# The last product of w_down in PSUM banks of its own, and the last output row gathered in one tile

## The chip, the core and the metric

The kernel runs on one core of one Trainium2 chip. Five engines work side by side: PE (TensorE, the matrix products; PEld is its weight load), DVE (VectorE), ACT (ScalarE), POOL (GpSimd) and SP (SyncE, which here only starts DMAs). The metric is the device time of one execution in microseconds (us); lower is better.

## The reference, cut to what matters

One encoder layer on 512 rows of 1024 numbers, all float32: two mixers, a cross-attention, then a SwiGLU feed-forward part and a final norm. Only the end bears on the change:

```python
def rms_norm(x, g):
    y = xf * lax.rsqrt(jnp.mean(xf * xf, axis=-1, keepdims=True) + EPS)
    return y * g
...
h = h + (silu(hn @ w_gate) * (hn @ w_up)) @ w_down      # hn (512, 1024), D_FF = 2816
return rms_norm(h, final_norm_g)
```

## The kernel before

**Tiles.** The residual `h` lies in SBUF as four tiles of 128 rows ("rows 0 to 3", index `t`) by 1024 columns; `HALF[0]` and `HALF[1]` are columns 0:512 and 512:1024. Every float32 operand of a product is split into a coarse half (`hi`, an ACT cast) and a remainder (`lo`, a DVE subtraction; `split`, lines 85 and 86), and `mm3` (line 374) issues three matmuls, hi by hi, hi by lo and lo by hi, for each 128x128 by 128x512 piece.

**w_down by seven products.** The 512x2816 by 2816x1024 product is done by Strassen's scheme with seven half-sized products in the order `DOWN = (1, 5, 2, 6, 3, 7, 4)`. Each goes through w_down in six chunks `c`, the sixth half as deep as the others. `down_product` runs a product into a pair of PSUM banks, one bank for each of two rows; `onto_h` (line 1922) then adds or subtracts a pair onto half a column range of two rows of `h`. The pairs are `dx`, `dq` and `dv`, six of the eight banks. The line that the text calls "the switch" stands where product 7 ends and product 4 begins:

```python
    down_product(dx, 7, False)
    onto_h(dx, 2, 0, ALU.subtract)
```

Product 4 goes on accumulating in `dx`: its sum with what `dx` already holds is what columns 512:1024 of rows 2 and 3 need, while `dx` up to product 7 is what is subtracted from columns 0:512.

**Product 4 and its order.** Chunks 0 to 2 run for both rows. Chunks 3 to 5 are held back (`HELD = 3`): row 2 is finished first, then row 3 in two column pieces of 256 in the banks `dv`. `seed_last` (line 1890) puts `h` plus the half-done bank into `dv` ahead of that; line 1959 adds row 2's bank onto `h`.

**Weights on their way.** A chunk is loaded by SP into one of three buffers `wraw` (line 299), cast by ACT into one of three `whi` buffers, and subtracted by DVE into one of three `wlo` buffers. A `wraw` buffer is free when DVE's subtraction has read it; a `whi` buffer when PE's last matmul on it is through. Chunk 3 of product 4 so takes the buffers of chunk 0, chunk 4 those of chunk 1, chunk 5 those of chunk 2. SP starts the loads in order, each when its buffer is free, and behind the last of them four stores of rows 0 and 1 (line 1950).

**Final norm.** `first_half` squares and multiplies by the gain the half of a row that is done first, and keeps the product in `hg`, four slots of 512 columns at the end of the tile `rest`, slot `t` for row `t`. `finish` or `finish_last` takes the other half, `inv_root` makes one over the root of the mean square, `write` scales both halves and stores them. For row 3 `write` has ACT scale `hg` (line 1906, 512 columns), DVE scale `h` (line 1914, 512 columns), SP store the one half (line 1912) and ACT's queue the other (line 1917).

**Order.** Outside the passages marked `in_order` a scheduler sorts each engine's instructions by its own model; `in_order` pins an instruction to the program's order.

Of the kernel before, what the change touches and what calls it, by code (L numbers as in the profile page):

```python
# [11 lines left out]
AF = mybir.ActivationFunctionType  # L12
ALU = mybir.AluOpType
# [4 lines left out]
P = 128  # L18
D = 1024
T = 512  # L20
NT = T // P
# [31 lines left out]
def hybrid_layer_kernel(  # L53
# [8 lines left out]
    nc = tc.nc  # L62
    x, mem, out = x[0], mem[0], out[0]
# [13 lines left out]
    def bank(name):  # L77
        return pm.tile([P, 512], F32, tag="mm", name=name)

    def aux(name, shape=(P, 512)):  # L80
        return pa.tile(list(shape), F32, tag="aux", name=name)
# [12 lines left out]
    in_order = tc.keep_in_program_order  # L94
# [165 lines left out]
    DOWN, CHUNKS = (1, 5, 2, 6, 3, 7, 4), 6  # L260
# [85 lines left out]
    def next_w(*key):  # L346
        i = used_w[0]
        used_w[0] += 1
        assert len(plan[i][0]) == len(key) and plan[i][0][1:] == key[1:] and plan[i][0][0] is key[0]
        for j in range(i, min(i + FAR + 1, len(plan))):  # L350
            begin(j, i)
            if j - 1 >= len(tiles) and j - 1 <= i + SPLITS:
                split_w(j - 1)
        for j in range(len(tiles), min(i + SPLITS + 1, len(plan))):
            split_w(j)
        tile_, tiles[i] = tiles[i], None
        return tile_
# [13 lines left out]
    def mm3(ps, a, b, start, stop, free=False, turn=False):  # L371

        for i, (x, y) in enumerate(((0, 0), (0, 1), (1, 0))):
            m = nc.tensor.matmul(ps, a[x], b[y], start=start and i == 0, stop=stop and i == 2, skip_group_check=free)  # L374
            if turn:
                in_order(m)
# [90 lines left out]
    def tick(us=5.2):  # L467

        side["now"] += us / 5.2
        run_due()  # L470
        side["credit"] = min(side["credit"] + us * side["rate"], us)
        while side["credit"] > 0.0 and side["gen"] is not None:
            try:
                used = next(side["gen"])
            except StopIteration:
                side["gen"] = None
                return
            if used is None:
                side["credit"] = 0.0
                return  # L480
            side["credit"] -= used

    def gain(src, name, late=False):
        t = np_.tile([P, D], F32, tag="gain", name=name, bufs=2)
        load = nc.sync.dma_start(t, src.partition_broadcast(P))
        if late:
            in_order(load)
        return t
# [8 lines left out]
    def sum_sq(dst, src, sq=None, bias=0.0):  # L497
        if sq is None:
            sq = np_.tile([P, 512], F32, tag="ev", name="sq", bufs=2)
        act = nc.scalar.activation(sq[:, :src.shape[-1]], src, AF.Square, bias=bias, accum_out=dst)  # L500
        if pinned[0]:
            in_order(act)
# [11 lines left out]
    HALF = (slice(0, 512), slice(512, 1024))  # L514
# [39 lines left out]
    def slot(tag, shape, dt, name, place=NEAR):  # L554
        n = math.prod(shape[1:])
        t = sp.tile([P, KD * T + ROOM[tag]], dt, tag=tag, name=name)[:, place[tag]:place[tag] + n]
        return t.rearrange("p (a b c) -> p a b c", a=shape[1], b=shape[2]) if len(shape) == 4 else (
            t.rearrange("p (a b) -> p a b", a=shape[1]))
# [838 lines left out]
    h = slot("A", (P, NT, D), F32, "h")  # L1397
# [242 lines left out]
    scaled = {}  # L1640
# [153 lines left out]
    def rows_product(ps, q, c, ops_, ts, cs, start, stop, turn=False):  # L1794
        hi, lo = ops_
        a = made[q, c // 2]
        for t in ts:
            tsl = slice(t * P, (t + 1) * P)
            for k in range(hi.shape[1]):
                kk = 2 * (c % 2) + k  # L1800
                mm3(ps[t], (a[0][:, kk, tsl], a[1][:, kk, tsl]), (hi[:, k, cs], lo[:, k, cs]),
                    start and k == 0, stop and k == hi.shape[1] - 1, True, turn)
        tick(1.35 * len(ts))

    def down_product(ps, q, start, chunks=range(CHUNKS)):
        for c in chunks:
            rows_product(ps, q, c, next_w(w_down, q, c), (0, 1), slice(0, 512), start and c == 0, c == CHUNKS - 1,
                         chunks[0] == c > 0)

    for i, u in enumerate(UNITS):  # L1810
        final = i == len(UNITS) - 1
        x, v = begun
# [13 lines left out]
        else:  # L1826
            dx = [bank(f"dx{t}") for t in range(2)]
# [20 lines left out]

    g_o = gain(final_norm_g, "g_o")
    hg = rest[0][:, 4:8, :]  # L1850
    msq = fp.tile([P, NT + 2], F32, name="msq", bufs=1)

    def mean_sq(dst, ss, base):
        nc.vector.scalar_tensor_tensor(dst, ss, 1.0 / D, base, ALU.mult, ALU.add)

    early, HELD = {}, 3

    def first_half(t, half):

        early[t] = half  # L1860
        sum_sq(hss[:, 2, t, half:half + 1], h[:, t, HALF[half]])
        nc.vector.tensor_tensor(hg[:, t, :], h[:, t, HALF[half]], g_o[:, HALF[half]], ALU.mult)
        nc.vector.tensor_scalar(msq[:, t:t + 1], hss[:, 2, t, half:half + 1], 1.0 / D, EPS, ALU.mult, ALU.add)

    def inv_root(t, ss):
        r = np_.tile([P, 1], F32, tag="r", name="r", bufs=2)
        ms = np_.tile([P, 1], F32, tag="ms", name="ms", bufs=2)
        root = nc.scalar.activation(ms, ss, AF.Sqrt, bias=msq[:, t:t + 1], scale=1.0 / D)
        inv = nc.vector.reciprocal(r, ms)
        if pinned[0]:  # L1870
            in_order(root)
            in_order(inv)
        return r
# [11 lines left out]
    last = [dv[i][:, 0:256] for i in range(2)]  # L1885
    last_cols = [slice(512 + 256 * i, 768 + 256 * i) for i in range(2)]

    def seed_last(ps):
        for i in range(2):
            in_order(nc.vector.tensor_tensor(last[i], h[:, NT - 1, last_cols[i]], ps[:, 256 * i:256 * i + 256], ALU.add))  # L1890

    def finish_last(i):
        ss = np_.tile([P, 2], F32, tag="ss", name="ss", bufs=2)
        sum_sq(ss[:, 0:1], last[i])
        in_order(nc.vector.tensor_tensor(h[:, NT - 1, last_cols[i]], last[i], g_o[:, last_cols[i]], ALU.mult))
        if i == 0:
            mean_sq(msq[:, NT:NT + 1], ss[:, 0:1], msq[:, NT - 1:NT])
        else:
            write(NT - 1, inv_root(NT, ss[:, 0:1]))

    stores = []

    def write(t, r):
        rows = out[t * P:(t + 1) * P]
        cs, hs = HALF[early[t]], HALF[1 - early[t]]
        scaled = nc.scalar.activation(hg[:, t, :], hg[:, t, :], AF.Copy, scale=r)
        if t < 2:
            nc.vector.scalar_tensor_tensor(h[:, t, hs], h[:, t, hs], r, g_o[:, hs], ALU.mult, ALU.mult)
            stores.extend([(rows[:, cs], hg[:, t, :]), (rows[:, hs], h[:, t, hs])])
            return  # L1910
        in_order(scaled)
        nc.sync.dma_start(rows[:, cs], hg[:, t, :])
        if t == NT - 1:
            in_order(nc.vector.tensor_scalar(h[:, t, hs], h[:, t, hs], r, None, ALU.mult))
        else:
            in_order(nc.vector.scalar_tensor_tensor(h[:, t, hs], h[:, t, hs], r, g_o[:, hs], ALU.mult, ALU.mult))
        (nc.scalar if t == NT - 1 else nc.sync).dma_start(rows[:, hs], h[:, t, hs])

    def onto_h(ps, t0, half, op):
        for t in range(2):  # L1920
            hs = h[:, t0 + t, HALF[half]]
            nc.vector.tensor_tensor(hs, hs, ps[t], op)  # L1922

    dq = [bank("dq0"), aux("dq1")]
# [7 lines left out]
    for t in range(2):  # L1932
        first_half(t, 1)
# [5 lines left out]
        finish(t)  # L1939
    down_product(dx, 7, False)  # L1940
    onto_h(dx, 2, 0, ALU.subtract)
    for t in range(2, 4):
        first_half(t, 0)

    held = []
    for c in range(CHUNKS):
        ops_ = next_w(w_down, 4, c)
        if c == CHUNKS - 1 - LOADS:
            for dst, src in stores:
                in_order(nc.sync.dma_start(dst, src))  # L1950
        if c < CHUNKS - HELD:
            rows_product(dx, 4, c, ops_, (0, 1), slice(0, 512), False, c == CHUNKS - HELD - 1)
        else:
            held.append((c, ops_))
    seed_last(dx[1])
    for c, ops_ in held:
        rows_product(dx, 4, c, ops_, (0,), slice(0, 512), False, c == CHUNKS - 1, True)
    pinned[0] = True
    in_order(nc.vector.tensor_tensor(h[:, 2, HALF[1]], h[:, 2, HALF[1]], dx[0], ALU.add))
    finish(2)  # L1960
    for i in range(2):
        for c, ops_ in held:
# [36 lines left out]
```

## Time and profile before

| | us |
|---|---|
| median of 3 runs | 866.23 (866.2, 866.23, 868.49) |
| the profiled execution, its own time | 865.49 |
| its span, first to last instruction | 863.7 |
| PE busy | 856.1 |
| DVE busy | 660.5 |
| ACT busy | 466.1 |

The granted TensorE clock of the profiled execution is 0.998. A row of the timeline begins with the start and the duration in us, then engine, line, operation and "output<-inputs"; a time in brackets is how long the engine sat idle before it and what ended that. A matmul row's duration is longer than the distance to the next one, since matmuls overlap; rates are read from starts.

### The profile page before, as it was taken

The page shows a single profiled execution, that of the slowest core. Times are in us where ns is not written, and L with a number is a line of the kernel's source. Part 1 is how long each engine was busy: PE and PEld are TensorE (multiplying, and loading weights), DVE is VectorE, ACT ScalarE, POOL GpSimd, SP SyncE. Part 2 cuts the span into 40 slices and gives each one's busy share as a digit, 9 for nine tenths or more (in the row PEclk, how much of TensorE's full clock was granted, in tenths as well). Part 3 has the DMA queues.
Part 4 walks back from the last instruction along what each step waited for, and adds up shares of the span by engine and source line. Part 5 has one row for each costly group of instructions (what it writes and reads, how often), then busy time and mean ns, then how long its engine had stood idle before and what let it go on. Part 6 is the DMA issues. An engine that isn't in the chain of part 4 may idle for free.

```text
span 863.7 us, 14764 instructions
## 1 busy us (share of the span) xinstructions
PE 856.1 (99%) x5780; PEld 766.6 (89%) x5780; DVE 660.5 (76%) x1076; ACT 466.1 (54%) x698; POOL 89.3 (10%) x119
## 2 busy tenths in 40 slices
PE   9999999999999999999999999999999999999997
PEld 7888888888889988889899888999999999988886
DVE  7698896899846768668758755867877768899875
ACT  6734853244355543557547544645545554656674
POOL 0002302111021110110010001010211111000000
PEclk9999999999999999999999999999999999999999
DMA  9759565987574798735696555557999898366564
GB/s 270 196 174 308 113 174 153 254 195 191 146 220 150 244 309 248 244 102 199 213 276 162 147 146 147 146 159 185 213 233 240 215 229 220 92 191 209 196 186 156
DMA packets 115752, 169.56 MB, mean 196 GB/s; under 512 B 9297, under 2 KB 80481, under 8 KB 115554
## 3 DMA queue, kind: packets, MB, share of 16 engines
q1 hardware_dynamic: 95330, 139.54, 49.3%
q0 software_dynamic: 20064, 28.55, 20.4%
q8 instruction: 45, 0.74, 0.3%
q10 hardware_dynamic: 288, 0.52, 0.2%
q14 instruction: 25, 0.20, 0.1%
HBM read 159.71 MB, written 48.73 MB: 241 GB/s over the span
## 4 chain that ended last, share of the span: by engine, by line
PE 99%; DVE 1%; ACT 0%; issue 0%
PE pf L374 27%; PE pt L374 18%; PE px L1238 13%; PE dx L374 7%; PE pq L1238 6%; PE dq L374 3%; PE pv L1238 3%; PE bx L1238 3%; PE qx L1238 3%; PE dv L374 2%; PE pz L958 2%; PE qv L1238 1%; PE po L374 1%; PE psc L374 1%; PE py L1014 1%; PE qq L1238 1%
## 5 line engine op out<-in xcount | busy, mean ns | idle before, releaser
L85 ACT CAST whi<-wraw 128x1024 fp32r<-128x1024 f32 x141 | 145.2, 1031 | 160.2 <-PE pf L374 54.8
L86 DVE TENSOR_TENSOR wlo<-wraw,whi 128x1024 fp32r<-128x1024 f32 x141 | 168.3, 1195 | 64.8 <-ACT whi L85 64.2
L374 PE MATMUL pf<-xn,whi 128*128 128x512 f32 x448 | 140.1, 392 | 0.0
L374 PEld LDWEIGHTS pf<-xn,whi 128*128 128x128 f32 x448 | 83.5, 188 | 16.9
L374 PE MATMUL pf<-xn,wlo 128*128 128x512 f32 x224 | 87.5, 391 | 0.0
L1238 PE MATMUL px<-fn,whi 128*128 128x256 f32 x480 | 83.4, 277 | 0.0
L1238 PEld LDWEIGHTS px<-fn,whi 128*128 128x128 f32 x480 | 72.5, 188 | 0.2
L86 DVE TENSOR_TENSOR wlo<-b,whi 128x1024 fp32r<-128x1024 f32 x40 | 48.9, 1223 | 26.0 <-ACT whi L85 26.0
L85 ACT CAST whi<-b 128x1024 fp32r<-128x1024 f32 x40 | 42.2, 1054 | 48.3 <-PE px L1238 27.7
L1238 PE MATMUL px<-fn,wlo 128*128 128x256 f32 x240 | 66.4, 277 | 0.0
L1238 PE MATMUL pq<-s,whi 128*128 128x256 f32 x320 | 55.0, 276 | 0.0
L374 PE MATMUL dx<-whi,s 128*128 128x512 f32 x166 | 52.2, 391 | 0.4 <-DVE h L1922 0.4
L86 DVE TENSOR_TENSOR wlo<-t,whi 128x1024 fp32r<-128x1024 f32 x30 | 36.7, 1225 | 18.4 <-ACT whi L85 18.4
L85 ACT CAST whi<-t 128x1024 fp32r<-128x1024 f32 x30 | 31.6, 1054 | 34.6 <-PE pv L1238 11.4
L374 PEld LDWEIGHTS pf<-xn,wlo 128*128 128x128 f32 x224 | 42.1, 188 | 8.7
L1238 PEld LDWEIGHTS pq<-s,whi 128*128 128x128 f32 x320 | 48.2, 188 | 0.0
L1238 PEld LDWEIGHTS px<-fn,wlo 128*128 128x128 f32 x240 | 45.1, 188 | 0.0
L1238 PE MATMUL pq<-s,wlo 128*128 128x256 f32 x160 | 44.2, 276 | 0.0
L374 PE MATMUL pt<-whi,xn 128*128 128x512 f32 x128 | 43.1, 402 | 0.0
L374 PEld LDWEIGHTS dx<-whi,s 128*128 128x128 f32 x166 | 31.1, 188 | 7.4 <-ACT whi L85 0.8
L374 PE MATMUL dx<-wlo,s 128*128 128x512 f32 x83 | 32.2, 389 | 0.0
L289 POOL DMA_DIRECT2D dsum<-in_w_down_dram x12 | 13.2, 1103 | 172.5 <-DMA dsum<-in_w_down_dram 167.4
(458 smaller groups left out, 2222.7 us busy)
## 6 DMA issues: line engine op xcount, KB each, us to landing
wraw<-in_w_in_dram SPq DMA_DIRECT2D x34, 512.0 KB, 4.6
dsum<-in_w_down_dram SPq DMA_DIRECT2D x20, 512.0 KB, 5.8
wraw<-dsum SPq DMA_DIRECT2D x20, 512.0 KB, 4.4
b<-in_w_gate_dram SPq DMA_DIRECT2D x15, 512.0 KB, 5.1
b<-in_w_up_dram SPq DMA_DIRECT2D x15, 512.0 KB, 4.7
wraw<-in_w_down_dram SPq DMA_DIRECT2D x15, 512.0 KB, 3.8
dsum<-in_w_down_dram POOLq DMA_DIRECT2D x10, 512.0 KB, 7.5
dsum<-dsum POOLq DMA_DIRECT2D x10, 512.0 KB, 7.9
```

The source lines that it names most:

```text
L85: hi = nc.scalar.copy(dst_hi, src)
L86: lo = nc.vector.tensor_tensor(dst_lo, src, dst_hi.bitcast(F32), ALU.subtract)
L289: plan[j + step][1].append((0, lambda d=dst, x=more: nc.gpsimd.dma_start(d, x, accum_op=ALU.add)))
L374: m = nc.tensor.matmul(ps, a[x], b[y], start=start and i == 0, stop=stop and i == 2, skip_group_check=free)
L958: nc.tensor.matmul(ps[:, g, :], wt[:, g, :], u[:, o * GO + g, :], start=True, stop=True)
L1014: in_order(nc.tensor.matmul(ps[64 * j:64 * j + 64, :, :, h, :].rearrange("p q d c -> p d q c"), a, b, start=k == ks[0], stop=k == ks[2], t ...
L1238: nc.tensor.matmul(ps[:, j, :], a[x], b[y], start=start and j == k == i == 0, stop=k == 3 and i == 2, skip_group_check=True)
```

## The change

Product 4 gets the pair `dq`, which product 3 has long left, and starts it afresh. What `dx` holds at the switch is now added onto columns 512:1024 of rows 2 and 3 as well, by two more DVE additions next to the two subtractions. `seed_last` and line 1959 read `dq` in place of `dx`. Row 3 is gathered in one tile: `hg`'s slots are dealt out by `HG` so that row 3's first half lies in slot 1 and its second half goes to slot 2, where row 0's half was, which the store of line 1950 (now 1960) has to have read by then. A new function `write_last` scales columns 0:352 of it on ACT and 352:1024 on DVE, and stores these two parts, SP the narrow one and ACT's queue the wide one. Line numbers behind it move up by 3 to 10.

```diff
+    HG = (2, 3, 0, 1)
+    last_row = hg[:, 1:3, :].rearrange("p a c -> p (a c)")
+    CUT = 352
...
-        nc.vector.tensor_tensor(hg[:, t, :], h[:, t, HALF[half]], g_o[:, HALF[half]], ALU.mult)
+        nc.vector.tensor_tensor(hg[:, HG[t], :], h[:, t, HALF[half]], g_o[:, HALF[half]], ALU.mult)
...
-        in_order(nc.vector.tensor_tensor(h[:, NT - 1, last_cols[i]], last[i], g_o[:, last_cols[i]], ALU.mult))
+        in_order(nc.vector.tensor_tensor(last_row[:, last_cols[i]], last[i], g_o[:, last_cols[i]], ALU.mult))
...
-            write(NT - 1, inv_root(NT, ss[:, 0:1]))
+            write_last(inv_root(NT, ss[:, 0:1]))
...
+    def write_last(r):
+        rows = out[(NT - 1) * P:NT * P]
+        x, y = last_row[:, 0:CUT], last_row[:, CUT:D]
+        in_order(nc.scalar.activation(x, x, AF.Copy, scale=r))
+        in_order(nc.vector.tensor_scalar(y, y, r, None, ALU.mult))
+        nc.sync.dma_start(rows[:, 0:CUT], x)
+        nc.scalar.dma_start(rows[:, CUT:D], y)
...
     down_product(dx, 7, False)
     onto_h(dx, 2, 0, ALU.subtract)
+    onto_h(dx, 2, 1, ALU.add)
...
-            rows_product(dx, 4, c, ops_, (0, 1), slice(0, 512), False, c == CHUNKS - HELD - 1)
+            rows_product(dq, 4, c, ops_, (0, 1), slice(0, 512), c == 0, c == CHUNKS - HELD - 1)
...
-    seed_last(dx[1])
+    seed_last(dq[1])
     for c, ops_ in held:
-        rows_product(dx, 4, c, ops_, (0,), slice(0, 512), False, c == CHUNKS - 1, True)
+        rows_product(dq, 4, c, ops_, (0,), slice(0, 512), False, c == CHUNKS - 1, True)
...
-    in_order(nc.vector.tensor_tensor(h[:, 2, HALF[1]], h[:, 2, HALF[1]], dx[0], ALU.add))
+    in_order(nc.vector.tensor_tensor(h[:, 2, HALF[1]], h[:, 2, HALF[1]], dq[0], ALU.add))
```

The scheduler sorts the passage around the switch anew. PE's order there before; `dx0` is row 2's bank, `dx1` row 3's, `whi_8860` is chunk 5 of product 7, `whi_8881`, `whi_8899` and `whi_8924` are chunks 0, 1 and 2 of product 4, and `s` holds the tokens:

```order
L374 MATMUL dx1_8077<-whi_8860,s4_8837 128x512
L374 MATMUL dx0_8076<-whi_8881,s1_8878 128x512
L374 MATMUL dx0_8076<-wlo_8882,s1_8878 128x512
L374 MATMUL dx0_8076<-whi_8881,s1_8878 128x512 x2
L374 MATMUL dx0_8076<-wlo_8882,s1_8878 128x512
L374 MATMUL dx0_8076<-whi_8881,s1_8878 128x512
L374 MATMUL dx0_8076<-whi_8899,s1_8878 128x512
L374 MATMUL dx0_8076<-wlo_8900,s1_8878 128x512
L374 MATMUL dx0_8076<-whi_8899,s1_8878 128x512 x2
L374 MATMUL dx0_8076<-wlo_8900,s1_8878 128x512
L374 MATMUL dx0_8076<-whi_8899,s1_8878 128x512
L374 MATMUL dx0_8076<-whi_8924,s2_8921 128x512
```

Row 2 takes chunks 0 and 1 in full before row 3 begins. The same place after the change, with `dq0` and `dq1` for rows 2 and 3:

```order
L374 MATMUL dx1_8077<-whi_8860,s4_8837 128x512
L374 MATMUL dq0_8217<-whi_8881,s1_8878 128x512
L374 MATMUL dq1_8218<-whi_8881,s1_8878 128x512
L374 MATMUL dq0_8217<-wlo_8882,s1_8878 128x512
L374 MATMUL dq0_8217<-whi_8881,s1_8878 128x512 x2
L374 MATMUL dq0_8217<-wlo_8882,s1_8878 128x512
L374 MATMUL dq0_8217<-whi_8881,s1_8878 128x512
L374 MATMUL dq1_8218<-wlo_8882,s1_8878 128x512
L374 MATMUL dq1_8218<-whi_8881,s1_8878 128x512 x2
L374 MATMUL dq1_8218<-wlo_8882,s1_8878 128x512
L374 MATMUL dq1_8218<-whi_8881,s1_8878 128x512
L374 MATMUL dq0_8217<-whi_8899,s1_8878 128x512
```

Both rows now go through chunk 0 before chunk 1. DVE's order from the switch to the subtraction of chunk 4 before:

```order
L1922 TENSOR_TENSOR h_3612<-h_3612,dx0_8076 128x512
L86 TENSOR_TENSOR wlo_8900<-wraw_8876,whi_8899 128x1024
L1922 TENSOR_TENSOR h_3612<-h_3612,dx1_8077 128x512
L1862 TENSOR_TENSOR rest_7714<-h_3612,g_o_8212 128x512
L86 TENSOR_TENSOR wlo_8925<-wraw_8897,whi_8924 128x1024
L86 TENSOR_TENSOR s4_8960<-rest_7714,s4_8960 128x512
L86 TENSOR_TENSOR s4_8960<-pair_5661,s4_8960 128x256
L1862 TENSOR_TENSOR rest_7714<-h_3612,g_o_8212 128x512
L1863 TENSOR_SCALAR msq_8214<-hss_3624 128x1 x2
L86 TENSOR_TENSOR wlo_8943<-wraw_8919,whi_8942 128x1024
L86 TENSOR_TENSOR wlo_8966<-wraw_8940,whi_8965 128x1024
```

and after the change, where `wlo_8900`, `wlo_8927`, `wlo_8945` and `wlo_8968` are the remainders of chunks 1, 2, 3 and 4:

```order
L1931 TENSOR_TENSOR h_3612<-h_3612,dx0_8076 128x512 x2
L86 TENSOR_TENSOR wlo_8900<-wraw_8876,whi_8899 128x1024
L1931 TENSOR_TENSOR h_3612<-h_3612,dx1_8077 128x512 x2
L1865 TENSOR_TENSOR rest_7714<-h_3612,g_o_8212 128x512
L86 TENSOR_TENSOR wlo_8927<-wraw_8897,whi_8926 128x1024
L86 TENSOR_TENSOR s4_8962<-rest_7714,s4_8962 128x512
L86 TENSOR_TENSOR s4_8962<-pair_5661,s4_8962 128x256
L1866 TENSOR_SCALAR msq_8214<-hss_3624 128x1
L1865 TENSOR_TENSOR rest_7714<-h_3612,g_o_8212 128x512
L86 TENSOR_TENSOR wlo_8945<-wraw_8921,whi_8944 128x1024
L1866 TENSOR_SCALAR msq_8214<-hss_3624 128x1
L86 TENSOR_TENSOR wlo_8968<-wraw_8942,whi_8967 128x1024
```

One addition stands ahead of chunk 1's subtraction and two ahead of chunk 2's. On ACT the square of row 3's first half moves behind the cast of chunk 3. Ahead of the switch every engine's order is as it was.

More of the change, by code (lines that the diff above doesn't have):

```diff
@@ L1905, in write @@
         cs, hs = HALF[early[t]], HALF[1 - early[t]]
-        scaled = nc.scalar.activation(hg[:, t, :], hg[:, t, :], AF.Copy, scale=r)
+        hgt = hg[:, HG[t], :]
+        scaled = nc.scalar.activation(hgt, hgt, AF.Copy, scale=r)
         if t < 2:
             nc.vector.scalar_tensor_tensor(h[:, t, hs], h[:, t, hs], r, g_o[:, hs], ALU.mult, ALU.mult)
-            stores.extend([(rows[:, cs], hg[:, t, :]), (rows[:, hs], h[:, t, hs])])
+            stores.extend([(rows[:, cs], hgt), (rows[:, hs], h[:, t, hs])])
             return
         in_order(scaled)
[L1912 to L1917, printed above, removed]
+        nc.sync.dma_start(rows[:, cs], hgt)
+        in_order(nc.vector.scalar_tensor_tensor(h[:, t, hs], h[:, t, hs], r, g_o[:, hs], ALU.mult, ALU.mult))
+        nc.sync.dma_start(rows[:, hs], h[:, t, hs])
+    def write_last(r):
[5 more added lines that the diff above has]
+        nc.scalar.dma_start(rows[:, CUT:D], y)
     def onto_h(ps, t0, half, op):
```

## The prediction

> **What bounds the kernel now.** I read the page first: who is busy, and who makes up the chain that ended last.
>
> ```profile
> PE 856.1 (99%) x5780; PEld 766.6 (89%) x5780; DVE 660.5 (76%) x1076; ACT 466.1 (54%) x698; POOL 89.3 (10%) x119
> PE 99%; DVE 1%; ACT 0%; issue 0%
> ```
>
> PE is the bound. No engine's order changes ahead of the switch, so only the last 22 us can move. For them I asked for the chain of waits from 838 us on (start, duration, what):
>
> ```profile
> 837.89 3.87 PE dx L374 x17
> ...
> 841.78 0.70 DVE h L1922
> ...
> 842.62 11.84 PE dx L374 x51
> ...
> 859.12 0.72 ACT rest L1906
> ```
>
> PE leaves the chain twice: at the switch, where DVE's subtraction of row 2's `dx` bank stands between two matmuls, and at the end, where the last row is scaled and stored. The change touches both. PE's timeline at product 7's first matmul, its last one, the first of product 4 and the first and last on `dv`:
>
> ```profile
> 827.08 0.62 PE L374 MATMUL dx<-whi,s 128*128 128x512 f32 x2
> ...
> 841.81 0.39 PE L374 MATMUL dx<-whi,s 128*128 128x512 f32 x1
> 842.62 0.47 PE L374 MATMUL dx<-whi,s 128*128 128x512 f32 x1 [0.42 <-DVE h L1922]
> ...
> 854.30 0.28 PE L374 MATMUL dv<-whi,s 128*128 128x256 f32 x1
> ...
> 857.77 0.28 PE L374 MATMUL dv<-whi,s 128*128 128x256 f32 x1
> ```
>
> Product 7 has 66 matmuls, 65 distances: (841.81 - 827.08) / 65 = 0.2266 us each. Without a wait product 4 would start at 842.04; it starts at 842.62, 0.58 later. Its 51 wide matmuls then take 854.30 - 842.62 = 11.68 us, 0.2290 each, where 51 x 0.2266 = 11.56: another 0.12 lost after the stop.
>
> **Part 1: two fresh banks.** DVE's timeline has the last reading of `dq`, by line 1922 on product 3, and the remainder of product 4's chunk 0:
>
> ```profile
> 828.57 0.68 DVE L1922 TENSOR_TENSOR h<-h,dq 128x512 f32<-128x512 f32 x1
> ...
> 839.29 1.23 DVE L86 TENSOR_TENSOR wlo<-wraw,whi 128x1024 fp32r<-128x1024 f32 x1 [1.35 <-ACT whi L85]
> ```
>
> Both are done by 840.52, the cast of that chunk ahead of its remainder, so the first matmul of product 4 finds a free bank and its weights at 842.04. PE should run through: `dv` starts at 842.04 + 51 x 0.2266 = 853.60 instead of 854.30, a gain of 0.70. Its bounds are 0.42 (the idle time that the row itself shows) and 0.81 (the whole distance 841.81 to 842.62).
>
> **Part 2: two more additions on DVE.** They are queued ahead of the remainders that product 4 needs. DVE's timeline from the switch on:
>
> ```profile
> 841.78 0.69 DVE L1922 TENSOR_TENSOR h<-h,dx 128x512 f32<-128x512 f32 x1
> 842.39 1.22 DVE L86 TENSOR_TENSOR wlo<-wraw,whi 128x1024 fp32r<-128x1024 f32 x1
> 843.52 0.68 DVE L1922 TENSOR_TENSOR h<-h,dx 128x512 f32<-128x512 f32 x1
> 844.12 0.69 DVE L1862 TENSOR_TENSOR rest<-h,g_o 128x512 f32<-128x512 f32 x1
> 844.72 1.22 DVE L86 TENSOR_TENSOR wlo<-wraw,whi 128x1024 fp32r<-128x1024 f32 x1
> ...
> 846.80 0.68 DVE L1862 TENSOR_TENSOR rest<-h,g_o 128x512 f32<-128x512 f32 x1
> ...
> 848.37 2.59 DVE L86 TENSOR_TENSOR wlo<-wraw,whi 128x1024 fp32r<-128x1024 f32 x2 [0.77 <-ACT whi L85]
> 851.75 0.69 DVE L86 TENSOR_TENSOR wlo<-wraw,whi 128x512 fp32r<-128x512 f32 x1 [0.79 <-ACT whi L85]
> 852.36 0.75 DVE L1890 TENSOR_TENSOR dv<-h,dx 128x256 f32<-128x256 f32 x2
> ```
>
> An addition takes 0.60 from start to start (843.52 to 844.12), a remainder 1.13. In the new order chunk 1's remainder ends at 842.39 + 0.60 + 1.22 = 844.21, chunk 2's at 844.72 + 1.20 + 1.22 = 847.14. PE asks for them at its 15th and 27th matmul, 842.04 + 14 x 0.2266 = 845.21 and 842.04 + 26 x 0.2266 = 847.93: 1.0 and 0.8 spare. For chunk 3's remainder DVE was free from 848.37 - 0.77 = 847.60 on; 1.20 later is 848.80, and it ends at 850.02; PE asks at its 38th, 850.42: 0.4 spare. The 0.77 and 0.79 us that DVE sat idle before take up the additions.
>
> For this chunk 3's cast must come sooner than it did. ACT's timeline (the casts of chunks 3 and 5), then SP's loads of chunks 4 and 5 with the time from issue to landing of each, from the answer on the tile `wraw` in a window round each:
>
> ```profile
> 847.29 1.05 ACT L85 CAST whi<-wraw 128x1024 fp32r<-128x1024 f32 x1 [1.93 <-issue]
> ...
> 851.10 0.62 ACT L85 CAST whi<-wraw 128x512 fp32r<-128x512 f32 x1 [1.39 <-PE dx L374]
> ...
> 843.63 0.32 SPq L299 DMA_DIRECT2D wraw<-dsum  x1
> DMA to landing us min/median/max: 4.4/4.4/4.4
> ...
> 845.97 0.32 SPq L299 DMA_DIRECT2D wraw<-dsum  x1
> DMA to landing us min/median/max: 4.0/4.0/4.0
> ```
>
> Before, row 3's chunk 0 stood 13 matmuls late in PE's order, and the cast at 847.29 waited for its buffer till then. Now chunk 0 is through after 12 matmuls, near 845.0, about when chunk 3's load lands; the cast ends near 846.1. Chunk 4's load starts behind chunk 1's remainder, at 844.22, and lands at 848.66; cast by 849.8, remainder by 851.2, wanted at 851.8. Chunk 5's load starts behind chunk 2's remainder, at 847.16 and not 845.97, and lands at 851.15; cast 851.2 to 851.85, remainder to 852.65, wanted at 842.04 + 49 x 0.2266 = 853.14: 0.5 spare. Line 1890 then ends at 853.4; its first piece, wanted at 853.60, at 853.0. So I take 0 for this part. The price if the cover is gone: every us by which chunk 5's load lands behind about 851.55 stops PE for a us.
>
> The four stores that SP starts behind that load go 1.2 later too. Line 1898 newly waits for the first of them, because row 0's half lay in slot 2; queued behind it on DVE are row 3's remaining operations, and the end waits for those. Both answers (stores of the whole run, DVE's timeline):
>
> ```profile
> DMA to landing us min/median/max: 2.1/2.5/4.7
> ...
> 857.68 0.42 DVE L1895 TENSOR_TENSOR h<-dv,g_o 128x256 f32<-128x256 f32 x1 [0.36 <-ACT sq L500]
> ```
>
> Even at 4.7 the store issued near 847.5 lands at 852.2, well ahead of 857.0. Cost 0.
>
> **Part 3: the tail.** What follows PE's last matmul moves with it by 0.70. Only the scaling and the two stores change. DVE's and ACT's scaling and the two issues, then the landing of ACT's store and of both together; the last two rows are groups of lines of the whole run, for the slopes (count, then busy, mean ns):
>
> ```profile
> 859.12 0.49 DVE L1914 TENSOR_SCALAR h<-h,r 128x512 f32<-128x512 f32 x1
> 859.12 0.72 ACT L1906 ACTIVATE rest<-rest,r 128x512 f32<-128x512 f32 x1 [0.23 <-DVE r L1869]
> 859.64 0.36 ACTq L1917 DMA_DIRECT2D out_dram<-h  x1
> 859.87 0.33 SPq L1912 DMA_DIRECT2D out_dram<-rest  x1
> ...
> DMA to landing us min/median/max: 2.1/2.1/2.1
> DMA to landing us min/median/max: 2.1/2.3/2.5
> ...
> L1520 DVE TENSOR_SCALAR prob<-prob,rs 128x256 f32<-128x256 f32 x16 | 4.9, 349 | 0.1
> L1142 ACT ACTIVATE zt<-zt,nm,r 128x1024 f32<-128x1024 f32 x4 | 5.0, 1244 | 0.9 <-DVE nm L1141 0.7
> ```
>
> DVE: (487 - 349) / 256 = 0.54 ns a column (0.49 is 487 in the grouped rows), so 672 columns take 0.49 + 160 x 0.00054 = 0.57. ACT: (1244 - 720) / 512 = 1.02 ns, so 352 columns take 0.72 - 0.16 = 0.56. Both end together. Beside the moved clock, SP's issue comes 0.16 earlier and ACT's 0.08 later, and the narrow store is now SP's, the wide one ACT's. The bytes are the same 512 KB. The last landing before was SP's, 859.87 + 2.5; a gain of 0.16 if the last issue sets the end, a loss of 0.08 if ACT's wide store ends last by its issue. I take a gain of 0.08, nearer to the first, since both stores move at once and their sum is unchanged.
>
> The Trainium skill (DMA: Bandwidth & Descriptors, Anatomy of one DMA) fits a DMA of GpSimd's path as 2.0 us plus its bytes over 436 GB/s, which speaks against a wider last store; by that estimate ACT's 336 KB would land 2.79 us after issue, a loss of 0.04 against SP's 256 KB before, and the sum would be 0.66. This case's 256 KB stores landed at 2.1 and 2.5, where it says 2.6.
>
> **Sum.** 0.70 + 0 + 0.08 = 0.78 off the profiled execution's own 865.49: 864.71. The median of the runs shown lies 0.74 higher, so on its scale 866.23 - 0.78 = 865.45, say 865.5.
>
> **The rivals.**
>
> *The cover is thin.* Chunk 5's load or DVE's queue comes 0.3 to 0.5 late and takes back half: 865.9. For it: spares of 0.4 and 0.5, worked out from single rows. Against it: the first bites only if DVE's queue is later than its old spacing says, the second only if the load is slower than its old self.
>
> *The stop has a second cause.* The idle time is put down to the last releaser only; if the switch also waited for weights, nothing is gained: 866.2. Against it: chunk 0's remainder was done at 840.52.
>
> *Slower: the last load.* The mechanism is chunk 5's load, 1.2 later behind chunk 2's remainder. It decides from a landing past 851.55 + 0.78 = 852.3, 5.2 us after issue, on. The same loads near the end, and the page's row for SP's loads from w_down into dsum, which are slower:
>
> ```profile
> DMA to landing us min/median/max: 3.2/3.8/4.8
> dsum<-in_w_down_dram SPq DMA_DIRECT2D x20, 512.0 KB, 5.8
> ```
>
> At 4.8 it costs 0.4 (the rival before). At 5.8 it lands at 852.97, PE stops 1.42, and the time is 866.23 - 0.78 + 1.42 = 866.9. Against it: no load of the first row took so long.
>
> **How the numbers follow.** Forecast 0.63, thin cover 0.15, second cause 0.08, last load 0.08, anything else 0.06. About 0.3%, 2.6 us, is what a measurement of this kernel can tell from no change; the first four cases all lie within it. Only something unnamed leaves it: faster 0.02, slower 0.04, the rest 0.94. The forecast's own bounds are gains of 0.42 - 0.08 = 0.34 and 0.81 + 0.16 = 0.97, 865.3 to 865.9. Single executions before spread from 865.49 to 868.49, so 0.7 more below; upward the range takes in the rivals up to 866.9: 864.5 to 866.9.
>
> **What would show it.** Right: no idle time on PE at the switch, the first matmul on `dv` at 853.6, the last at 857.1; chunk 3's cast near 845, chunk 5's near 851.2; ACT's and DVE's last scaling ending within 0.05 of each other. Wrong: PE idle in front of chunk 3, 4 or 5, put down to DVE `wlo` or ACT `whi`; line 1898 waiting for a DMA; a last landing later after PE's end than the 4.6 us before (862.37 - 857.77).

## The result, and the profile after

The changed kernel takes 865.75 us (median of 19 runs, 864.21 to 867.22); the kernel before took 867.64 in the same comparison (19 runs, 865.68 to 870.25). The ratio is 0.9983, interval 0.9975 to 0.9991. The profiled execution took 865.99 us, its span 864.2, against 865.49 and 863.7 for the profiled execution before. That span is longer although the kernel is faster, because single executions of one kernel differ by 3 to 5 us (864.21 to 867.22 and 865.68 to 870.25 here). So I compare the two traces from one event on: the start of product 7's last matmul, after which everything that the change touches takes place. I call what follows "the stretch".

The busy times on the page of the changed kernel:

```profile
PE 856.6 (99%) x5780; PEld 766.9 (89%) x5780; DVE 661.8 (77%) x1078; ACT 465.7 (54%) x698; POOL 89.3 (10%) x119
```

Two DVE instructions more, 1.3 us of DVE's time. The chain of waits from 838 us on:

```profile
837.85 5.89 PE dx L374 x26
843.74 11.58 PE dq L374 x51
855.32 3.60 PE dv L374 x30
...
859.99 0.59 ACT rest L1923
```

Product 7, product 4 and the last two quarter rows follow each other on PE, and DVE's subtraction is gone from between them. The timeline of PE at the switch (start, duration):

```profile
843.35 0.39 PE L374 MATMUL dx<-whi,s 128*128 128x512 f32 x1
843.58 0.61 PE L374 MATMUL dq<-whi,s 128*128 128x512 f32 x2
```

The first matmul of product 4 starts 0.23 after product 7's last one, where it was 0.81. From 843.35 the stretch lasts 20.83 us; before, from 841.81, it lasted 863.69 - 841.81 = 21.88. The difference, 1.05 us, is 0.12% of the time, a ratio of 0.9988, which lies inside the measured interval.

In the table, which I made from the traces, all times are us after the start of product 7's last matmul. SP's and ACT's landing are those of the last two stores by the queue that carries them.

```
kernel                        first p4  first dv  last dv  SP lands  ACT lands  end
before                          0.81     12.49     15.96     20.55     19.88    21.88
changed                         0.23     11.81     15.28     19.49     19.93    20.83
changed, second profile         0.23     11.79     15.26     19.51     19.91    20.84
changed, third profile          0.23     11.79     15.26     19.54     19.92    20.88
banks only                      0.23     11.79     15.26     19.85     19.18    21.18
tail only                       0.81     12.49     15.96     20.18     20.61    21.52
additions late                  0.23     11.79     15.26     19.52     19.91    20.86
stores swapped                  0.23     11.79     15.26     19.82     19.99    21.33
four additions more             0.23     13.05     16.52     20.80     21.18    22.13
cut at 512                      0.23     11.79     15.26     19.85     19.17    21.19
one store                       0.23     11.79     15.26      -        19.90    20.81
additions late and one store    0.23     11.96     15.43      -        20.07    20.98
```

Of the 1.05, PE gives 0.68 (the start of the last `dv` matmul, 15.96 to 15.28). After PE, the end came 5.92 later and now comes 5.55 later, a gain of 0.37, although the last landing (20.55 - 15.96 = 4.59 before, 19.93 - 15.28 = 4.65 now) comes no earlier. The tail gained more than was forecast, and the last landing is not what gained it.

The waits that end the program, on SP's own queue, before and then after (engine and line, for what, us in total, times, longest):

```profile
SPq L1994 <- DMA out_dram<-rest: 2.0, 1, 2.0
...
SPq L1994 <- PEq L1994: 0.7, 2, 0.5
```

```profile
SPq L2004 <- DMA out_dram<-rest: 1.8, 1, 1.8
...
SPq L2004 <- PEq L2004: 0.7, 2, 0.5
```

Only one store makes SP wait in either kernel, for 2.0 us before and 1.8 now. The 0.7 us put down to PE's sequencer (PEq) are the same in both and come behind the last store's wait. SP's records at the end, which these rows sum up, show why the tail gained:

```
before:   first wait ends 862.37, then 862.44, 862.50, 862.56, 862.62, 862.68, 862.74, 862.80; end 863.69
          SP's store landed 862.36, ACT's 861.69
changed:  first wait ends 862.86, then 862.93, 862.99, 863.05, 863.11, 863.17, 863.23, 863.29; end 864.19
          SP's store landed 862.85, ACT's 863.28
waited for, in both:      semaphores 100, 102, 104, 106, 107, 108, 109, 110
raised, in both:          100 by SP's store of row 3, 110 by ACT's
```

SP works through a row of eight waits, one after the other, 0.06 us each. A semaphore is a counter that a landed DMA raises, and these eight belong to the DMAs of SP and ACT. So the first wait is for SP's store of row 3, the eighth for ACT's. In both kernels the first of the row ends 0.02 after SP's own store lands, and the seven others follow at their fixed distance; from SP's landing to the end of the span it is 1.34 us. Before, ACT's store had long landed, and the whole row came behind SP's. In the changed kernel ACT's wide store lands 0.43 after SP's narrow one, at 863.28, and the eighth wait ends at 863.29. From ACT's landing to the end it is only 0.91. The row of seven waits, 0.43 us, now lies beside ACT's store instead of behind the last landing. The 1.34 of the kernel before gives the end of the changed one: 19.49 + 1.34 = 20.83. ACT's landing is no later than that end allows, but only just: in the second and third profile the eighth wait ends 0.04 and 0.06 after it.

### The profile page after: what moved, and what is told of

It is laid out like the page before. It is cut to its first block, busy times and chain, and to the rows that moved or that the text cites. A ratio compares the mean times of both kernels' runs of the same rounds, so it can differ in the third digit from the quotient of the medians.

```text
span 864.2 us, 14766 instructions
## 1 busy us (share of the span) xinstructions
PE 856.6 (99%) x5780; PEld 766.9 (89%) x5780; DVE 661.8 (77%) x1078; ACT 465.7 (54%) x698; POOL 89.3 (10%) x119
## 4 chain that ended last, share of the span: by engine, by line
PE 95%; DMA 2%; DVE 2%; issue 0%; ACT 0%; ACTq 0%; DVEq 0%
PE pf L374 26%; PE pt L374 15%; PE px L1238 13%; PE pq L1238 6%; PE dx L374 5%; PE dq L374 5%; PE pv L1238 3%; PE bx L1238 3%; PE qx L1238 3%; PE dv L374 2%; DMA ed<-e 1%; PE pz L958 1%; PE qv L1238 1%; PE po L374 1%; PE psc L374 1%; PE py L1014 1%
## 5 line engine op out<-in xcount | busy, mean ns | idle before, releaser
L374 PE MATMUL dx<-whi,s 128*128 128x512 f32 x132 | 41.4, 390 | 0.0
L374 PE MATMUL dq<-whi,s 128*128 128x512 f32 x122 | 38.0, 389 | 0.0
L1238 PEld LDWEIGHTS pq<-s,wlo 128*128 128x128 f32 x160 | 30.1, 188 | 0.0
```

The costliest lines, as they stand in the source:

```text
L1238: nc.tensor.matmul(ps[:, j, :], a[x], b[y], start=start and j == k == i == 0, stop=k == 3 and i == 2, skip_group_check=True)
```

## The experiments

The theory: PE gained what the prediction says, 0.70 by the free banks; the tail gained about 0.36 because SP's store, which the row of waits meets first, became narrow and landed earlier. The rivals: the tail's gain comes from something else in it (the one tile, the queues, the last landing); the additions still cost something that another gain hides; and, since 0.9983 is a little more than 0.9988, something beyond the stretch became faster.

**The changed kernel again**, the same code, on the chip of the next three.

> The changed kernel itself, again, beside its parts. From the last matmul of product 7 to the end of the span it took 20.83 us in its first profile, 21.88 before. Theory (two parts): 0.68 of the 1.05 comes from PE running through the switch, 0.37 from the tail; the time is 1.05 us under the kernel before, ratio 0.9988, and the stretch from the switch is 20.8 again. Rival (something ahead of the switch also got faster, since the 19 runs gave 1.5): ratio 0.9983 or less with the same 20.8.

866.45 against 867.59, ratio 0.9994, interval 0.9985 to 1.0003. The stretch is 20.84, the first profile's to 0.01, and 20.88 in the third profile further down. So one profile's stretch is good to about 0.05 us here, while the whole time of 11 runs doesn't tell 1 us from nothing.

**Banks only**: the kernel before, with product 4 in `dq` and the two additions.

```diff
+    onto_h(dx, 2, 1, ALU.add)
...
-            rows_product(dx, 4, c, ops_, (0, 1), slice(0, 512), False, c == CHUNKS - HELD - 1)
+            rows_product(dq, 4, c, ops_, (0, 1), slice(0, 512), c == 0, c == CHUNKS - HELD - 1)
...
```

> Only product 4 in dq and the two more additions; the last row is scaled and stored as before. Theory (two parts): no stop at the switch, last matmul on dv 15.28 us behind the last of product 7, the tail behind it as before, so 21.88 - 0.68 = 21.2 from the switch to the end; ratio 0.9992. Rival (the banks do it all): 20.8, ratio 0.9988.

Ratio 0.9993, interval 0.9982 to 1.0003, and the stretch ends at 21.18, 0.70 sooner than before. Its chain of waits:

```profile
837.79 5.89 PE dx L374 x26
843.68 11.56 PE dq L374 x51
855.24 3.60 PE dv L374 x30
```

From product 4's first start to the first on `dv` it is 11.56 us, which is 51 x 0.2266 to the hundredth, where it was 11.68 before. The stop and the slow restart are both gone (before, the first distance behind the stop was 0.31 in place of 0.2266), so the two additions cost PE nothing in this execution. Nothing else moved, since SP's and ACT's landings move by the same 0.70.

**Tail only**: the kernel before, with row 3 in one tile and cut at 352.

```diff
+    HG = (2, 3, 0, 1)
+    last_row = hg[:, 1:3, :].rearrange("p a c -> p (a c)")
+    CUT = 352
...
-            write(NT - 1, inv_root(NT, ss[:, 0:1]))
+            write_last(inv_root(NT, ss[:, 0:1]))
...
```

> Only the last row in one tile and the cut at 352; product 4 stays in dx. Theory (two parts): PE stops 0.58 at the switch as before, last matmul on dv at 15.96, but the end at 21.88 - 0.37 = 21.5, because SP's row of waits at the end runs while ACT's wide store is still landing; ratio 0.9996. Rival (the banks do it all): 21.9, ratio 1.0000. Rival (a fit by bytes: a wider store lands later): 21.9 or more.

Ratio 0.9990, interval 0.9981 to 0.9999; the stretch ends at 21.52, 0.37 sooner. PE still stops at the switch:

```profile
843.19 0.39 PE L374 MATMUL dx<-whi,s 128*128 128x512 f32 x1
844.00 0.47 PE L374 MATMUL dx<-whi,s 128*128 128x512 f32 x1 [0.42 <-DVE h L1931]
```

0.81 from start to start, as before. The parts add up: 0.70 + 0.37 = 1.07 against 1.05, 1.04 and 1.01 for the whole change in its three profiles. So neither part hides a cost of the other beyond 0.06, and the tail is worth about 0.36.

**Additions late**: the changed kernel, with the two additions onto columns 512:1024 put behind the remainder of chunk 4.

```diff
...
-    onto_h(dx, 2, 1, ALU.add)
...
+        if c == CHUNKS - 2 - SPLITS:
+            rest_4 = rest_of[0]
...
+    onto_h(dx, 2, 1, ALU.add, rest_4)
...
```

> The changed kernel with the two more additions behind the remainder of chunk 4, where DVE was idle. Theory (the additions are covered, PE runs through anyway): 20.8 from the switch to the end, ratio as the changed kernel's within 0.0003, only the spares grow (chunk 3's remainder done 1.4 us ahead of PE instead of 0.2). Rival (thin cover: in some runs PE stops for chunk 3, 4 or 5): faster than the changed kernel by 0.2 to 0.5 us, with a narrower spread of its runs.

Ratio 0.9988, interval 0.9978 to 0.9997, stretch 20.86 against 20.83 to 20.88: no gain in the profiled executions. Whether PE stops in some others, as the rival has it, isn't settled: 0.9988 against 0.9994 for the changed kernel on the same chip is a step its way, but the intervals overlap. The timeline of DVE here, and that of the changed kernel's first profile:

```profile
849.63 2.37 DVE L86 TENSOR_TENSOR wlo<-wraw,whi 128x1024 fp32r<-128x1024 f32 x2
851.91 1.28 DVE L1934 TENSOR_TENSOR h<-h,dx 128x512 f32<-128x512 f32 x2
```

```profile
843.33 1.28 DVE L1931 TENSOR_TENSOR h<-h,dx 128x512 f32<-128x512 f32 x2
844.87 1.23 DVE L86 TENSOR_TENSOR wlo<-wraw,whi 128x1024 fp32r<-128x1024 f32 x1 [0.26 <-ACT whi L85]
846.01 1.28 DVE L1931 TENSOR_TENSOR h<-h,dx 128x512 f32<-128x512 f32 x2
...
847.81 1.22 DVE L86 TENSOR_TENSOR wlo<-wraw,whi 128x1024 fp32r<-128x1024 f32 x1
...
850.54 1.23 DVE L86 TENSOR_TENSOR wlo<-wraw,whi 128x1024 fp32r<-128x1024 f32 x1
...
851.74 1.86 DVE L86 TENSOR_TENSOR wlo<-wraw,whi 128x1024 fp32r<-128x1024 f32 x2
```

In the changed kernel the subtractions carry the additions along (843.33 and 846.01), and the remainders of chunks 1 to 5 end at 846.10, 849.03, 851.77, about 852.96 and 853.60. PE wants them at 843.58 + 14, 26, 37, 43 and 49 times 0.2266: 846.75, 849.47, 851.96, 853.32 and 854.68. The spares are 0.65, 0.44, 0.19, 0.36 and 1.08. At chunk 3, with 0.19, PE loses 0.02 over the five matmuls behind the one that needs the remainder, which is why `dv` starts at 11.81 in this profile and at 11.79 in the others.

This execution was the thin one. The changed kernel's second profile has the same order on DVE, at chunks 1 and 3:

```profile
844.58 1.22 DVE L86 TENSOR_TENSOR wlo<-wraw,whi 128x1024 fp32r<-128x1024 f32 x1
...
850.25 1.22 DVE L86 TENSOR_TENSOR wlo<-wraw,whi 128x1024 fp32r<-128x1024 f32 x1
```

The second and the third profile give spares of 1.0, 0.79, 0.55, 0.71 and 1.40. In them chunk 1's remainder starts 1.18 after product 7's last matmul, in the first profile 1.52, behind a later cast.

**Four additions more**: the changed kernel with the two additions taken off and put on once more, which leaves `h` the same but for rounding.

```diff
     onto_h(dx, 2, 1, ALU.add)
+    onto_h(dx, 2, 1, ALU.subtract)
+    onto_h(dx, 2, 1, ALU.add)
```

> The changed kernel with a subtraction and an addition more on each of the two rows (they cancel), which stand one each ahead of the remainders of chunks 2, 3, 4 and 5, 0.6 us each on DVE. Theory (the two additions are covered by 0.2 to 0.5 us ahead of chunk 3): 1.2 us more ahead of chunk 3's remainder stops PE for 0.7 to 1.0, 1.8 ahead of chunk 4's for some more; the end at 20.84 + 1.0 to 1.5, 21.8 to 22.3. Rival (DVE is far from the path): 20.8.

A single execution: 869.24 against 867.8 for one of the kernel before. The stretch ends at 22.13, 1.29 later than the changed kernel's second profile, and the last `dv` matmul starts 1.26 later. Waits from 838 to 866, then the chain:

```profile
PEld dq L374 <- DVE wlo L86: 1.5, 2, 0.9
...
PE dq L374 <- DVE wlo L86: 0.5, 1, 0.5
```

```profile
850.10 1.14 DVE wlo L86
...
855.23 1.14 DVE wlo L86
856.37 0.04 issue
856.41 2.11 PE dq L374 x8
858.52 3.60 PE dv L374 x30
```

Four operations of 0.60 more are 2.4 us of DVE's time, but only two stand ahead of chunk 3's remainder and three ahead of chunk 4's. PE stops for these two: from start to start 0.91 and 0.53 in place of 0.2266. The first stop, 0.68, fits the spare of 0.55 that the second and third profile show: 1.20 - 0.55 = 0.65. Behind each stop the next distance is 0.34, so about 0.1 more is lost on each restart, as at the switch of the kernel before. What would have cost is DVE's queue at the chunks with the smallest spares, and not chunk 5's load.

**Stores swapped**: the changed kernel, SP storing the wide part and ACT's queue the narrow one.

```diff
-        nc.sync.dma_start(rows[:, 0:CUT], x)
-        nc.scalar.dma_start(rows[:, CUT:D], y)
+        nc.sync.dma_start(rows[:, CUT:D], y)
+        nc.scalar.dma_start(rows[:, 0:CUT], x)
```

> The changed kernel with the two last stores on each other's queue: SP stores the wide part (672 columns), ACT's queue the narrow one. All times from the last matmul of product 7. Theory (the end is SP's own landing plus 1.33 us of SP's waits, or the landing on ACT's queue plus 0.90, whichever is later): SP's wide store lands near 19.9, the end at 21.2 to 21.3. Rival (the last landing sets the end, on whichever queue): 20.8. Rival (only the even scaling on ACT and DVE counts): 20.8.

A single execution: 867.55 against 867.8. The stretch ends at 21.33, 0.48 after the changed kernel's second profile. That is close to the number I had for it, but its reason was wrong: I had taken SP's own store to be the first of the row. Here the first wait ended at 864.46, 0.02 behind ACT's narrow store (864.44), while SP's wide one had landed at 864.28. The issues and SP's waits:

```profile
out_dram<-rest SPq DMA_DIRECT2D x1, 336.0 KB, 2.6
...
out_dram<-rest ACTq DMA_DIRECT2D x1, 176.0 KB, 2.8
```

```profile
SPq L2004 <- DMA out_dram<-rest: 2.3, 1, 2.3
```

Behind that wait the other seven run at their 0.06, and the end is 19.99 + 1.34 = 21.33. So the queue doesn't decide which store is waited for first. The records of SP and ACT say what does: their 321 DMAs raise the eight semaphores in turn, in the order of issue (two of the very first are swapped in some traces), and SP's row goes through the semaphores by number. The store of row 3 that is issued first raises 110, the eighth, and the one issued behind it (by 0.01 to 0.23 us) starts the next turn with 100, the first. In each kernel with two stores of row 3 the later one is the part that ACT scales. A kernel that issues them the other way round wasn't tried. And the narrow store doesn't land early on either queue: here it lands 0.16 behind the wide one, while in the changed kernel, on SP's queue, it lands 0.43 ahead.

**Cut at 512**: the changed kernel with equal halves in the one tile.

```diff
-    CUT = 352
+    CUT = 512
```

> The changed kernel with the cut at 512: last row still in one tile, two equal parts as before. Theory (SP's landing plus 1.33): ACT's scaling 0.72, SP's issue 0.13 later, its landing as before the change, the end at 21.2. Rival (the gain of the tail comes from the one tile, not from the cut): 20.8.

A single execution: 865.9 against 867.8. The stretch ends at 21.19, that of the kernel with the banks only (21.18); SP's half lands at 19.85, and 19.85 + 1.34 = 21.19. So one tile by itself gives nothing: the cut gives the whole gain of the tail, 0.35 here.

**One store**: the changed kernel, with the whole row stored in one DMA by ACT's queue.

```diff
-        nc.sync.dma_start(rows[:, 0:CUT], x)
-        nc.scalar.dma_start(rows[:, CUT:D], y)
+        nc.scalar.dma_start(rows, last_row)
```

> The changed kernel with one store of the whole last row (512 KB) on ACT's queue, scaled at the cut of 352 as before. Theory (SP's waits run while ACT's store lands, then 0.90): landing near 19.9 to 20.0, the end 20.8 to 20.9, though one store waits for both scalings and moves all the bytes. Rival (a fit by bytes, 0.4 us later for 176 KB more): landing 20.3, the end 21.2.

A single execution: 866.43 against 867.8; stretch 20.81. Its DMA issue, and the same answer for the changed kernel:

```profile
out_dram<-rest ACTq DMA_DIRECT2D x1, 512.0 KB, 2.6
```

```profile
out_dram<-rest ACTq DMA_DIRECT2D x1, 336.0 KB, 2.7
...
out_dram<-rest SPq DMA_DIRECT2D x1, 176.0 KB, 2.2
```

The one store of 512 KB lands at 19.90, as late as the last of the two (19.93), so here the last landing fits their bytes together rather than the wider store's own. And this store stands last in SP's row: with one DMA fewer it raises 110, the other waits were through by then, and 19.90 + 0.91 is the end. By the first place's 1.34 it would have been 21.24, an estimate that no run tested.

The Trainium skill (DMA: Bandwidth & Descriptors, Anatomy of one DMA) fits a DMA of GpSimd's path as 2.0 us plus its bytes over 436 GB/s; by that estimate these three would take 3.20, 2.79 and 2.41 us from issue to landing. These stores, which SP and ACT issue, took 2.63, 2.69 and 2.25 in the traces, and the measurement decides: the 512 KB store is no slower than the 336 KB one beside its neighbour.

**The changed kernel a third time, and both variants together** (additions late, one store), on another chip with the same runs of the kernel before, to see whether the first 0.9983 holds anything beyond the stretch, and whether the two variants make a better kernel.

> The changed kernel once more. The stretch from the last matmul of product 7 to the end says 1.04 us less than before, ratio 0.9988. Theory (that is all): ratio within 0.9980 and 0.9996. Rival (something more, as 0.9983 in the first 19 runs hinted): again 0.9983 or less.

> The changed kernel with both variants that cost nothing in their profiles: the additions behind chunk 4's remainder, and one store of the whole last row on ACT's queue. Theory (both are off the path): 20.8 from the last matmul of product 7 to the end, ratio as the changed kernel's on this chip within 0.0005. Rival (the wider spares show over many runs): 0.2 to 0.5 us faster than the changed kernel.

Ratios 0.9997 (0.9987 to 1.0006) and 0.9997 (0.9988 to 1.0006); stretches 20.88 and 20.98. The changed kernel's three ratios are 0.9983, 0.9994 and 0.9997, and 0.9988, the stretch's, is inside all three intervals: nothing beyond the stretch has been shown. The two variants together are no better, and their stretch is 0.10 longer. DVE in that kernel, with ACT's cast of chunk 1 ahead of it, then PE:

```profile
843.77 1.05 ACT L85 CAST whi<-wraw 128x1024 fp32r<-128x1024 f32 x1 [2.57 <-DMA wraw<-dsum]
...
844.85 1.23 DVE L86 TENSOR_TENSOR wlo<-wraw,whi 128x1024 fp32r<-128x1024 f32 x1 [1.38 <-ACT whi L85]
...
852.25 1.29 DVE L1933 TENSOR_TENSOR h<-h,dx 128x512 f32<-128x512 f32 x2
853.45 0.69 DVE L86 TENSOR_TENSOR wlo<-wraw,whi 128x512 fp32r<-128x512 f32 x1
```

```profile
854.22 0.48 PE L377 MATMUL dq<-wlo,s 128*128 128x512 f32 x1
```

`dv` starts 0.17 later than in the changed kernel. The load of chunk 1 landed late in this execution: ACT's cast stood 2.57 us for it and DVE 1.38 for the cast, so all that follows on DVE came late. Chunk 1's remainder was done 0.13 ahead of PE, and PE lost 0.08 behind it. Chunk 5's, with the additions ahead of it, ends at 854.14, and the matmul that needs it starts 0.08 later; the distance behind that one is 0.32 instead of 0.2266, another 0.09. In the kernel with the additions late alone the load came in time and neither happened. So a remainder that is done this shortly ahead of PE already costs some hundredths: 0.02 at 0.19 in the changed kernel's first profile, 0.08 at 0.13 here. No version measured beats the changed kernel by more than its own profiles differ.

## Why the prediction came out as it did

**The time.** 865.5 was forecast, 865.75 came, from a base of 866.23 that itself came out at 867.64 in the comparison. So the absolute time agrees partly by luck: the base came out 1.41 higher and the gain larger than forecast, and the two nearly cancel. The gain in the compared medians is 1.9 us, in the stretch 1.05, and 0.78 was forecast, with bounds of 0.34 to 0.97. The 0.3% that I took as what a measurement can tell from no change was too coarse: the interval of the 19 runs is 0.16% wide and leaves out 1, though those of the two later comparisons don't.

**Part 1, right.** 0.70 forecast, 0.68 in the changed kernel's first profile and 0.70 measured in all kernels with `dq` and no new stop. On the changed kernel's clock, 1.54 later than the one before (843.35 against 841.81), `dv` starts at 855.16 - 1.54 = 853.62, forecast 853.60, and its last matmul at 858.63 - 1.54 = 857.09, forecast 857.1. The distance of 0.2266 is what made this exact: the 0.12 of the restart could not be read from the idle time alone.

**Part 2, right in its cost.** 0 forecast; 0.02 in the changed kernel's first profile, nothing in its second and third and in the banks-only kernel. The spares forecast for chunks 1, 2, 3, 4 and 5 were 1.0, 0.8, 0.4, 0.6 and 0.5; in the second and third profile they are 1.0, 0.79, 0.55, 0.71 and 1.40, as forecast within 0.15 but for the last. In the first profile they are 0.65, 0.44, 0.19, 0.36 and 1.08. There the first four are 0.2 to 0.4 smaller, because chunk 1's remainder itself waited for its cast ("0.26 <-ACT whi"), and DVE's whole queue behind it moved by that. ACT's casts of chunks 1, 3 and 5 in it:

```profile
843.78 1.05 ACT L85 CAST whi<-wraw 128x1024 fp32r<-128x1024 f32 x1 [2.04 <-PE dx L374]
...
847.45 1.04 ACT L85 CAST whi<-wraw 128x1024 fp32r<-128x1024 f32 x1
...
852.25 0.63 ACT L85 CAST whi<-wraw 128x512 fp32r<-128x512 f32 x1 [1.57 <-DMA wraw<-dsum]
```

On the old clock chunk 3's cast starts at 845.91 and chunk 5's at 850.71, where 845 and 851.2 were forecast; in the second profile it is 845.17 and 850.40. In the first profile chunk 3's had its load in time; no idle time stands in its row, so other work on ACT came ahead of it, behind the late cast of chunk 1. Chunk 5's load took 3.1 us from issue to landing, where I had taken 4.0 and feared 5.2. The thin cover as a rival named two margins, DVE's queue with 0.4 and chunk 5's load with 0.5: the first was the real one, down to 0.19 in one of three profiles, the second never fell below 1.08 in them. Line 1898 waited for ACT's square, never for a store.

**Part 3, the step that failed.** The scalings came nearly as worked out: 0.59 on ACT (forecast 0.56) and 0.57 on DVE, both beginning at 859.99. ACT's slope of 1.02 ns a column came from two instructions that differ in more than columns, since line 1142 reads both `nm` and `r` beside its tile and line 1906 only `r`; from 0.72 at 512 columns to 0.59 at 352 it is 0.8. The issues moved as forecast: beside PE's 0.68 in this profile, SP's came 0.13 earlier and ACT's 0.08 later (0.16 and 0.08 forecast), by these rows:

```profile
860.59 0.38 ACTq L1926 DMA_DIRECT2D out_dram<-rest  x1
860.60 0.33 SPq L1925 DMA_DIRECT2D out_dram<-rest  x1
```

But the term was taken at 0.08, between bounds of a loss of 0.08 and a gain of 0.16, and it measured 0.35 to 0.37. The step that failed is that the issue or landing of the last store sets the end. The bounds were loose even so: a loss of 0.08 by ACT's issue leaves out that ACT's store had landed 0.67 ahead of SP's. In place of that step the runs show two conditions, of which the later counts: 1.34 us behind the store that SP waits for first, 0.91 behind the one it waits for last. Before, the first was the later; the cut lets the two meet. I had not followed SP's own waits behind the last store in the trace of before, where the 0.43 between the first and the last wait stands in SP's records.

The sign to watch for, "a last landing later after PE's end than the 4.6 us before", came true (4.65) and meant nothing: the end came sooner all the same.

**The rivals.** The second cause is out: no wait is left at the switch. The last load is out at 3.1 us: it landed at 850.60 on the old clock, where the cover would have ended near 851.6. The thin cover bit by 0.02 at most in the three profiles, but four more operations on DVE show that it would have cost 1.26 with 2.4 us more.

## What to carry to other kernels

Follow the trace past the last landing to the end of the span, and ask which store's wait comes first on the engine that closes the program: a store that lands a little sooner there can be worth more than the last landing. An idle time in a row is less than what the stop costs: measure from start to start against the steady distance. And where a gain is a thousandth of the time, compare the traces from one shared event on, and do each part of the change alone: 0.70 and about 0.36 were settled by single profiles, while the whole times of eleven runs each told them from nothing barely or not at all.

## What the runs showed of the hardware

I had not expected the row of eight waits at the program's end, 0.06 us each, in which a store's place counts: 1.34 us from the first-waited landing to the end in the kernel before, the cut at 512 and the swapped stores, 0.91 from the last-waited one in the changed kernel's first profile and with the single store. The place follows from the turn of the eight semaphores, so one DMA more or fewer in the program moves it: the last of 321 raises the first of the row, the last of 320 the eighth. Nor that 512 KB in one store lands 2.63 us after issue, when 336 KB beside 176 KB took 2.69. And where the scatter of 3 to 5 us between executions of one kernel comes from: with PE's instructions of the two first profiles laid on each other, the changed kernel is 0.6 us late at 5 us, 0.9 at 83 us and 1.5 at 414 us, long ahead of the switch, where both kernels run the same instructions; its second profile lies behind at other places (0.8 at 11 us, 1.7 at 531 us). At 414 us PE sat idle 0.51 us for ACT's cast of a chunk of w_v, and ACT 2.83 us for that chunk's load, where it had been 2.24 before. Why that load landed later, and what delayed the other places, stays open.
